# First feed-forward of a diffusion layer: quad weight pieces prepared in pairs in a written-out order, dot tiles loaded one piece ahead, SiLU rows kept in DRAM

## The chip, the cores and the metric

The kernel runs on 1 core of one Trainium2 chip. The metric is the device time of one execution in microseconds. The kernel before took 2806.91 us as the median of 3 runs (2805.06 to 2813.4).

## The reference, cut to what matters

The program is one layer on 256 latent and 256 context tokens of width 2048: a half-step SwiGLU, a token mixer (attention and a long convolution), and a second half-step SwiGLU. Each is modulated by shifts, scales and gates from one linear map `w_ada` of SiLU(c) for the latent tokens and of SiLU(c_ctx) for the context tokens.

```python
D_MODEL, SEQ, CTX_LEN, D_FF, N_MOD = 2048, 256, 256, 5632, 9

def half_ffn(s, m, slot, g, w_up, w_down):
    h = modulate(rms_norm(s, g), chunk(m, 3 * slot), chunk(m, 3 * slot + 1))
    gate, up = jnp.split(h @ w_up, 2, axis=-1)
    return s + 0.5 * chunk(m, 3 * slot + 2) * ((silu(gate) * up) @ w_down)

mod = (silu(c) @ w_ada + b_ada)[:, None, :]          # 9 chunks of 2048
mod_c = (silu(c_ctx) @ w_ada + b_ada)[:, None, :]
x = half_ffn(x, mod, 0, g_norm[0], w_ffn1_up, w_ffn1_down)
ctx = half_ffn(ctx, mod_c, 0, g_norm[0], w_ffn1_up, w_ffn1_down)
...                                                  # token mixing, then the second half_ffn on x
```

All values are 32-bit floats. The change lies in the two `half_ffn` lines of slot 0 (the first ff) and in the `w_ada` products that are computed beside them.

## The kernel before, in words

**Products in two parts.** A float operand is split into a high part `hi` (a cast to the matmul format fp32r, on ScalarE) and a remainder `lo = raw - hi` (on VectorE). One product of blocks is then three matmuls: hi by hi, hi by lo, lo by hi (`mm3`, L239 to L241). `split_to` (L208 cast, L209 remainder) and `weight` (L228 cast, L232 remainder) make the parts.

**The up loop.** The columns of `w_up` are worked in 44 steps j of 128 gate and 128 up columns. Steps 0 to 2 (the wave) run first, beside the start of the kernel. Steps 3 to 43 are `Ffn.up` (from 240 us to 1165 us in the profile nearly all of this loop). A step takes its 16 blocks of the inner dimension in four pieces kq of 4 blocks, each loaded as a tile `raw` of 128 x 1024 floats, 512 KB (`weight_load`, L216, SP's queue, 4 buffers).

- Piece kq = 0 is always plain. Its weights are cast into tiles `u` (L418, L419), and its remainder is made by an accumulating DMA from POOL's queue (L420). From j = 4 on its raw tile is `plain`, with one buffer. It is prepared one step ahead, after the products of kq = 1 of the step before.
- Pieces kq = 3, 2, 1 become quad pieces from j = 5, 7, 9 on. A quad piece computes its 2 x 2 x 2 block products with seven products instead of eight, on tokens of one stream (256 columns, where a plain product has both, 512). Its products come in two parts: first three products per block pair on the raw weights' first three blocks (the plain part, tiles `bhi`, `blo`, 128 x 768, 2 buffers each in the pool `adap`), then four on sums of the weights (the summed part, tiles `whi`, `wlo`, 128 x 1024, 3 buffers each). So a quad piece has 2 x 7 x 3 = 42 matmuls of 256 columns, and a plain piece 4 x 2 x 3 = 24 of 512.
- In `prepare`, a quad piece is made in this order: bhi (ScalarE), blo (VectorE), three in-place sums on `raw` (L426, L427, L428, VectorE), whi (ScalarE), wlo (VectorE).

At the end of a step its sums are combined on VectorE (L474 to L481, with a SiLU at L480 on ScalarE) into one tile of activations, and `keep` (L484 on) stores it to DRAM as a high part and a remainder: a cast, a negated copy, two stores and an accumulating store, all from POOL's queue (L489, L490, L491).

**The dots.** The products with `w_ada` that are not needed at once are made on VectorE: a tile `adaw` of 128 x 1024 weights (512 KB, L141, SP's queue) is multiplied by a SiLU row `crow`, replicated on all partitions, and summed along the row (L145). Columns 5 to 8 of the nine (`ADA_UP`, 128 dots) run in the up loop with 2 buffers, columns 2 to 4 (`ADA_DOWN`, two rows each) in the down loop with 4. `ada_hook` is called after each piece and adds a rate of 0.79 dots per call in the up loop; the load and its dot are written one right after the other (`ada_dve`). A load stands behind the latest weight load on SP's queue.

**The rows.** `open_dots` loads a row of 2048 floats of c into all partitions (1 MB, L896, ScalarE's queue) and applies SiLU there (L897, 128 x 2048): one row before the up loop, two before the down loop.

**The down loop** (about 1165 to 1700 us) reads the activations back (L506, POOL's queue) in groups of four j, from group 9 on, then 8, 10 and the others, with weights from `w_dn` (24 plain products per step).

**What sets the order.** The program is written in one sequence; the build gives each engine its own queue and may set an instruction earlier or later than its place in the text where its inputs allow. `tc.issue_after(x)` sets what is written inside it behind x on x's engine. Each engine and each DMA-issuing queue works its list in order. In the trace of before, for instance, the first dots run before the wave's activations, behind which they are written.

Of the kernel before, what the change touches and what calls it, by code (L numbers as in the profile page):

```python
# [14 lines left out]
ALU = mybir.AluOpType  # L15
# [47 lines left out]
def hybrid_layer_kernel(ctx: ExitStack, tc: tile.TileContext, a):  # L63
# [14 lines left out]
    def U(shape, dt=F32):  # L78
        return T(up, shape, "u", dt, 58)
# [50 lines left out]
    warm = mod[0][8][:, 0:1]  # L130
    S.activation(warm, ones[:, 0:1], AF.Silu)

    def ada_dve(c, d, b):
        n = c * KT + d
        t = T(adap, (P, D // 2), "adaw", bufs=adaw_bufs)
        src = a["w_adaT"][n, :, b * (D // 2) : (b + 1) * (D // 2)]
        if last_load[0] is None:
            nc.scalar.dma_start(t, src)
        else:
            with tc.issue_after(last_load[0].ins):  # L140
                nc.sync.dma_start(t, src)  # L141
        for i in range(2 if c < 5 else 1):
            sc = T(adap, (P, D // 2), "adas", mybir.dt.bfloat16, bufs=1)
            mcol = mod[i][c][:, d : d + 1]
            V.tensor_tensor_reduce(  # L145
                out=sc, in0=t, in1=crow[i][:, b * (D // 2) : (b + 1) * (D // 2)], scale=1.0,
                scalar=mcol if b else bada[:, n : n + 1], op0=ALU.mult, op1=ALU.add, accum_out=mcol,
            )

    def ada_finish(c, d0, d1):  # L150
        for i in range(2 if c < 5 else 1):
# [200 lines left out]
    class Ffn:  # L352
        def __init__(self, wup, wdown, cm, hook=None):
            self.wup, self.wdown, self.cm = wup, wdown, cm
            self.hook = hook or (lambda: None)
            self.h = [None] * KT
            self.mm = mm3
            self.held = {}
            self.sums, self.first = {}, {}
            self.wupq = a["w_up1q"]  # L360

        def open(self, alt=False):
# [47 lines left out]
        def prepare(self, j, kq):  # L410

            pool = adap if kq == 0 and j > WAVE else None
            raw = weight_load(self.wupq[j - WAVE, kq], (P, 2, 4, P), pool=pool)
            out = []
            if kq == 0:
                hi, lo = ([U((P, 4, P), F32R) for _ in range(2)] for _ in range(2))
                for q in range(2):
                    S.copy(hi[q], raw[:, q])  # L418
                    S.activation(lo[q], hi[q].bitcast(F32), AF.Copy, scale=-1.0)  # L419
                    nc.gpsimd.dma_start(lo[q], raw[:, q].bitcast(F32R), accum_op=ALU.add)  # L420
                return [(hi, lo)]
            if not self.quads(j, kq):
                return [weight(None, (P, 2, 4, P), raw=raw)]
            for n in (3, 4):
                if n == 4:
                    V.tensor_sub(raw[:, :, 0:4:3], raw[:, :, 3:4].broadcast_to((P, 2, 2, P)), raw[:, :, 0:3:2])  # L426
                    V.tensor_sub(raw[:, :, 2], raw[:, :, 2], raw[:, :, 0])  # L427
                    V.tensor_sub(raw[:, :, 1], raw[:, :, 1], raw[:, :, 2])  # L428
# [20 lines left out]
        def up(self, j):  # L449
# [2 lines left out]
            total = list(left)  # L452
            banks = [(PA, PB)[j % 2]((P, 2, L)) if n else None for n in left]
            for kq in range(4):
                w = self.prepare(j, kq) if kq else self.ahead
# [107 lines left out]
    NF = 64  # L563
    dram = ctx.enter_context(tc.tile_pool(name="dram", bufs=1, space=bass.MemoryType.DRAM))
    spec = [T(dram, (P, 2, L), f"spec{i}") for i in range(8)]
    actd = [T(dram, (P, 2, 2, L), f"act{j}", F32R) for j in range(JT)]

    def filter_spectrum():
# [108 lines left out]
    def ada_next():  # L677
        if done[0] < len(todo):
            c, d, b = todo[done[0]]
            ada_dve(c, d, b)  # L680
            done[0] += 1
            if b == 1:
                ada_finish(c, d, d + 1)

    def ada_hook():
        owed[0] += rate[0]
        while owed[0] >= 1.0:
            owed[0] -= 1.0
            ada_next()

    steps = filter_spectrum()
    load = None
# [196 lines left out]
    def open_dots(n, bufs):  # L889
        nonlocal adap, adap_cm, adaw_bufs  # L890
        adap_cm = tc.tile_pool(name="adap", bufs=2)
        adap, adaw_bufs = adap_cm.__enter__(), bufs
        crow.clear()
        for i in range(n):
            crow.append(T(adap, (P, D), f"crow{i}", bufs=1))
            nc.scalar.dma_start(crow[i], a["crow"][i : i + 1, :].partition_broadcast(P))  # L896
            S.activation(crow[i], crow[i], AF.Silu)  # L897

    adap = adap_cm = adaw_bufs = None
    open_dots(1, 2)  # L900

    xs = [[None] * (KT // 2) for _ in range(2)]
    build = f1.build()
# [2 lines left out]
    for j in range(WAVE, JT):  # L906
        f1.up(j)
        if j == WAVE:
            f1.hook = lambda: (next(build, None), ada_hook())
    rs1 = U((P, 2, L))  # L910
    cont, lat = [], []

# [3 lines left out]

    more = mix_input(1, cont, PASSES[-1][0], PA)
    norm_plan = iter(NORM_PLAN)
    while done[0] < len(ADA_UP) * KT * 2:
        ada_next()  # L920
    adap_cm.__exit__(None, None, None)
    open_dots(2, 4)
    owed[0] = -4.0

    def down_hook(p):
# [6 lines left out]
    while done[0] < len(todo):  # L932
        ada_next()
    last_load[0] = None
    adap_cm.__exit__(None, None, None)


    mp_cm = tc.tile_pool(name="mp", bufs=1)
# [671 lines left out]
```

## Time and profile before

| | |
|---|---|
| runs, median (range) | 2806.91 us (2805.06 to 2813.4) |
| the profiled execution | 2812.43 us |
| its span | 2810.7 us |
| granted TensorE clock, mean | 0.983 |
| DMA, mean over the span | 217 GB/s |
| issues of the up loop's raw, plain and dot tiles (each 512 KB, whole page) | 124, 40 and 223 |

The profile is of one execution. PE is TensorE's matmuls, PEld its weight loads, DVE VectorE, ACT ScalarE, POOL GpSimd, SP SyncE; "SPq" and the like is the engine's queue that issues DMAs. "L145" is a line of the kernel. In a group or a timeline row, "wlo<-raw,whi" names what is written and what is read; "x110" is a count; behind the bar or in brackets stands the time that the engine was idle just before, and what ended it. A line of waits gives the total in us, the number of times and the longest. The view of one line or tile gives shortest, median and longest duration in ns, and when the first and the last of them started.

### The profile page before, as it was taken

The page shows a single profiled execution, that of the slowest core. Times are in us where ns is not written, and L with a number is a line of the kernel's source. Part 1 is how long each engine was busy: PE and PEld are TensorE (multiplying, and loading weights), DVE is VectorE, ACT ScalarE, POOL GpSimd, SP SyncE. Part 2 cuts the span into 40 slices and gives each one's busy share as a digit, 9 for nine tenths or more (in the row PEclk, how much of TensorE's full clock was granted, in tenths as well). Part 3 has the DMA queues.
Part 4 walks back from the last instruction along what each step waited for, and adds up shares of the span by engine and source line. Part 5 has one row for each costly group of instructions (what it writes and reads, how often), then busy time and mean ns, then how long its engine had stood idle before and what let it go on. Part 6 is the DMA issues. An engine that isn't in the chain of part 4 may idle for free.

```text
span 2810.7 us, 37981 instructions
## 1 busy us (share of the span) xinstructions
PE 2653.9 (94%) x14480; PEld 2255.6 (80%) x14480; DVE 1914.2 (68%) x3050; ACT 1112.7 (40%) x1546; POOL 253.5 (9%) x394
## 2 busy tenths in 40 slices
PE   8999888898989988799999999999999999999999
PEld 5677788887878888687887798888878888888887
DVE  6756777767777767577897769688875545554444
ACT  5343333433433334311121145546554444444333
POOL 1121111111111111232001000000000000000000
PEclk9999999999999999899999999999999999999999
DMA  9976677777776777899678756633556666666665
GB/s 370 349 218 190 192 210 213 220 207 203 192 227 190 207 205 214 288 376 314 242 251 296 256 178 178 187 113 124 187 166 191 189 188 189 189 192 203 202 202 157
DMA packets 194146, 608.94 MB, mean 217 GB/s; under 512 B 22315, under 2 KB 25324, under 8 KB 189484
## 3 DMA queue, kind: packets, MB, share of 16 engines
q1 hardware_dynamic: 140012, 501.77, 54.2%
q0 software_dynamic: 53184, 100.95, 15.1%
q10 hardware_dynamic: 768, 3.80, 0.3%
q8 instruction: 113, 1.85, 0.3%
q14 instruction: 69, 0.57, 0.1%
HBM read 546.13 MB, written 38.81 MB: 208 GB/s over the span
## 4 chain that ended last, share of the span: by engine, by line
PE 53%; issue 22%; DMA 14%; DVE 7%; POOL 3%; ACT 1%; SPq 0%; POOLq 0%; DVEq 0%; ACTq 0%
PE pa L1270 9%; PE pa L1271 9%; PE pa L1269 9%; DMA adaw<-in_w_adaT_dram 6%; PE pa L247 3%; DMA act<-u 3%; PE pb L241 3%; PE pb L239 3%; PE pb L240 3%; DVE adas L145 2%; PE pa L239 2%; PE pa L240 2%; PE pa L241 2%; DMA u<-plain 2%; PE pa L249 2%
## 5 line engine op out<-in xcount | busy, mean ns | idle before, releaser
L232 DVE TENSOR_TENSOR wlo<-raw,whi 128x1024 fp32r<-128x1024 f32 x487 | 595.0, 1223 | 415.6 <-ACT whi L228 414.2
L228 ACT CAST whi<-raw 128x1024 fp32r<-128x1024 f32 x487 | 511.9, 1052 | 882.9 <-PE pa L1271 413.4
L1269 PE MATMUL pa<-whi,u 128*128 128x512 f32 x1060 | 414.1, 391 | 0.6 <-ACT whi L228 0.6
L1270 PE MATMUL pa<-wlo,u 128*128 128x512 f32 x1060 | 412.9, 390 | 0.5 <-DVE wlo L232 0.5
L1271 PE MATMUL pa<-whi,u 128*128 128x512 f32 x1060 | 412.9, 390 | 0.0
L239 PE MATMUL pa<-u,whi 128*128 128x256 f32 (+1 forms) x928 | 318.3, 344 | 32.9 <-ACT whi L208 21.5
L241 PE MATMUL pa<-u,wlo 128*128 128x256 f32 (+1 forms) x928 | 316.2, 341 | 24.1 <-DVE wlo L209 20.6
L241 PE MATMUL pb<-u,wlo 128*128 128x256 f32 (+1 forms) x920 | 310.8, 338 | 23.1 <-DVE wlo L209 14.5
L239 PE MATMUL pb<-u,whi 128*128 128x256 f32 (+1 forms) x920 | 311.2, 338 | 17.2 <-ACT whi L208 17.1
L240 PE MATMUL pa<-u,whi 128*128 128x256 f32 (+1 forms) x928 | 314.2, 339 | 4.5 <-DMA u<-act 4.1
L240 PE MATMUL pb<-u,whi 128*128 128x256 f32 (+1 forms) x920 | 307.7, 334 | 0.0
L145 DVE CUSTOM_DVE_ANT_0 adas<-adaw,crow,mod 128x1024 bf16<-128x1024 f32 x160 | 205.2, 1283 | 130.7 <-DMA adaw<-in_w_adaT_dram 128.3
L145 DVE CUSTOM_DVE_ANT_0 adas<-adaw,crow,cond 128x1024 bf16<-128x1024 f32 x160 | 205.1, 1282 | 127.2 <-DMA adaw<-in_w_adaT_dram 116.4
L208 ACT CAST whi<-raw 128x1024 fp32r<-128x1024 f32 x111 | 116.3, 1048 | 430.5 <-DVE raw L428 430.5
L1270 PEld LDWEIGHTS pa<-wlo,u 128*128 128x128 f32 x1060 | 199.1, 188 | 41.8 <-DVE wlo L232 1.0
L1269 PEld LDWEIGHTS pa<-whi,u 128*128 128x128 f32 x1060 | 199.0, 188 | 41.7 <-ACT whi L228 1.1
L1271 PEld LDWEIGHTS pa<-whi,u 128*128 128x128 f32 x1060 | 199.0, 188 | 41.3
L239 PEld LDWEIGHTS pa<-u,whi 128*128 128x128 f32 x928 | 180.1, 194 | 60.2 <-ACT whi L208 24.6
L241 PEld LDWEIGHTS pa<-u,wlo 128*128 128x128 f32 x928 | 180.5, 195 | 47.4 <-DVE wlo L209 25.5
L241 PEld LDWEIGHTS pb<-u,wlo 128*128 128x128 f32 x920 | 179.0, 195 | 46.6 <-DVE wlo L209 19.3
L239 PEld LDWEIGHTS pb<-u,whi 128*128 128x128 f32 x920 | 178.9, 194 | 37.8 <-ACT whi L208 20.2
L240 PEld LDWEIGHTS pa<-u,whi 128*128 128x128 f32 x928 | 180.5, 195 | 23.4 <-DMA u<-act 5.7
(353 smaller groups left out, 4725.0 us busy)
## 6 DMA issues: line engine op xcount, KB each, us to landing
adaw<-in_w_adaT_dram SPq DMA_DIRECT2D x223, 512.0 KB, 5.8
raw<-in_w_dn_dram SPq DMA_DIRECT2D x184, 512.0 KB, 3.7
raw<-in_w_up_dram SPq DMA_DIRECT2D x176, 512.0 KB, 3.6
raw<-in_w_up1q_dram SPq DMA_DIRECT2D x124, 512.0 KB, 5.4
u<-act POOLq DMA_DIRECT2D x136, 256.0 KB, 9.0
act<-u POOLq DMA_DIRECT2D x132, 256.0 KB, 3.8
wrow<-in_w_ada_dram SPq DMA_DIRECT2D x32, 1024.0 KB, 9.7
plain<-in_w_up1q_dram SPq DMA_DIRECT2D x40, 512.0 KB, 3.7
```

Source lines behind the costliest of these rows:

```text
L145: V.tensor_tensor_reduce(out=sc, in0=t, in1=crow[i][:, b * (D // 2) : (b + 1) * (D // 2)], scale=1.0, scalar=mcol if b else bada[:, n : n ...
L208: S.copy(hi, src)
L228: S.copy(hi, raw)
L232: V.tensor_sub(lo, raw, hi.bitcast(F32))
L239: PE.matmul(ps, w[0], xx[0], start=start, stop=False)
L240: PE.matmul(ps, w[0], xx[1], start=False, stop=False)
L241: return PE.matmul(ps, w[1], xx[0], start=False, stop=stop)
L247: PE.matmul(ps, w[0], x, start=start, stop=stop)
L249: PE.matmul(ps[:, 0, :], w[1], x[:, 0, :], start=False, stop=False)
L1269: PE.matmul(ps[t], hi, w[0], start=start, stop=False)
L1270: PE.matmul(ps[t], hi, w[1], start=False, stop=False)
L1271: last = PE.matmul(ps[t], lo, w[0], start=False, stop=stop)
```

## The change

Four things change.

1. **Quad pieces in pairs.** `prepare` returns the raw tile of a quad piece, and the new `quad_weights` does the rest. For a piece n it also begins the next quad piece n+1, perhaps of the next step: its load, its plain cast and its plain remainder. The order is given: on ScalarE the plain cast of n+1, then the summed cast of n; on VectorE the plain remainder of n+1, then the summed remainder of n, then the sums of n+1.
2. **Dots one piece behind their loads.** `ada_hook` issues the load; the dot is written at the next call, and behind the latest summed (or plain) remainder on VectorE (`last_lo`). The buffers stay 2 and 4. The hook makes no more than the up loop's 128 loads there; what is left is done by `dots_rest`.
3. **SiLU rows in DRAM.** Both rows are loaded once as a 32 x 128 tile (POOL's queue), one SiLU is applied, and they are stored to `silu_rows` in DRAM (POOL's queue). The replicated rows are read from there on SP's queue: row 0 once before the up loop, kept through the down loop, row 1 before the down loop.
4. **The last activation.** `keep` of j = 43 makes its parts by a cast and a VectorE remainder and stores them with two plain stores.

The core of the diff ("..." marks what is left out):

```diff
-    def ada_dve(c, d, b):
+    last_lo = [None]
+    waiting = []
+
+    def dot_load(c, d, b):
...
         if last_load[0] is None:
-            nc.scalar.dma_start(t, src)
+            nc.sync.dma_start(t, src)
...
+    def dot(t, c, d, b):
         for i in range(2 if c < 5 else 1):
...
+        if b == 1:
+            ada_finish(c, d, d + 1)
...
-            V.tensor_sub(lo, raw, hi.bitcast(F32))
+            last_lo[0] = V.tensor_sub(lo, raw, hi.bitcast(F32))
...
-            for n in (3, 4):
-                if n == 4:
-                    V.tensor_sub(raw[:, :, 0:4:3], raw[:, :, 3:4].broadcast_to((P, 2, 2, P)), raw[:, :, 0:3:2])
-                    V.tensor_sub(raw[:, :, 2], raw[:, :, 2], raw[:, :, 0])
-                    V.tensor_sub(raw[:, :, 1], raw[:, :, 1], raw[:, :, 2])
-                if n == 3:
-                    hi, lo = (T(adap, (P, 2, n, P), name, F32R, 2) for name in ("bhi", "blo"))
-                else:
-                    hi, lo = (T(wp, (P, 2, n, P), name, F32R, 3) for name in ("whi", "wlo"))
-                out.append(split_to(raw[:, :, 0:n], hi, lo))
-            return out
+            return raw
+
+        def plain_part(self, raw):
+            hi, lo = (T(adap, (P, 2, 3, P), name, F32R, 2) for name in ("bhi", "blo"))
+            return raw, hi, lo, S.copy(hi, raw[:, :, 0:3])
+
+        def remainder(self, raw, hi, lo):
+            return V.tensor_sub(lo, raw[:, :, 0:3], hi.bitcast(F32))
...
+        def quad_weights(self, j, kq):
+            if self.begun is None:
+                raw, hi, lo, _ = self.plain_part(self.prepare(j, kq))
+                self.remainder(raw, hi, lo)
+                self.sums_of(raw)
+                self.begun = raw, hi, lo
+            raw, hi, lo = self.begun
...
+            if n < JT * 4:
+                nraw, nhi, nlo, cast = self.plain_part(self.prepare(n // 4, n % 4))
+            thi, tlo = (T(wp, (P, 2, 4, P), name, F32R, 3) for name in ("whi", "wlo"))
+            with ExitStack() as order:
+                if cast is not None:
+                    order.enter_context(tc.issue_after(cast.ins))
+                S.copy(thi, raw)
+            if cast is not None:
+                rem = self.remainder(nraw, nhi, nlo)
+            with ExitStack() as order:
+                if cast is not None:
+                    order.enter_context(tc.issue_after(rem.ins))
+                last_lo[0] = V.tensor_sub(tlo, raw, thi.bitcast(F32))
+            if cast is not None:
+                then(last_lo[0], self.sums_of, nraw)
+                self.begun = nraw, nhi, nlo
+            return [(hi, lo), (thi, tlo)]
...
         def keep(self, j, act):
+            if j == JT - 1:
+                for s_, t in enumerate(split(act, (P, 2, L))):
+                    nc.gpsimd.dma_start(actd[j][:, s_], t)
+                return
...
+    def dots_due(keep):
+        while len(waiting) > keep:
+            t, step = waiting.pop(0)
+            with ExitStack() as order:
+                if last_lo[0] is not None:
+                    order.enter_context(tc.issue_after(last_lo[0].ins))
+                dot(t, *step)
+
     def ada_hook():
+        behind = len(waiting)
         owed[0] += rate[0]
-        while owed[0] >= 1.0:
+        while owed[0] >= 1.0 and done[0] < len(todo):
             owed[0] -= 1.0
-            ada_next()
+            dots_due(adaw_bufs - 1)
+            behind = min(behind, len(waiting))
+            waiting.append((dot_load(*todo[done[0]]), todo[done[0]]))
+            done[0] += 1
+        dots_due(len(waiting) - behind)
...
+    rows = T(up, (2 * KT, P), "mt", bufs=3)
+    nc.gpsimd.dma_start(rows, a["crow"].rearrange("i (k p) -> (i k) p", p=P))
     f1.ahead = f1.prepare(WAVE, 0)
     for j in range(WAVE):
         f1.close(j, wave[j])
+    S.activation(rows, rows, AF.Silu)
+    nc.gpsimd.dma_start(silu_rows.rearrange("i k p -> (i k) p"), rows)
...
+    def row_in(pool, i):
+        crow.append(T(pool, (P, D), f"crow{i}", bufs=1))
+        nc.sync.dma_start(crow[i], silu_rows[i : i + 1].rearrange("i k p -> i (k p)").partition_broadcast(P))
```

More of the change, by code (lines that the diff above doesn't have):

```diff
@@ L141, in ada_dve @@
                 nc.sync.dma_start(t, src)
+        return t
+    def dot(t, c, d, b):
         for i in range(2 if c < 5 else 1):
@@ L358, in __init__ @@
             self.held = {}
-            self.sums, self.first = {}, {}
+            self.sums, self.first, self.begun = {}, {}, None
             self.wupq = a["w_up1q"]
@@ L413, in prepare @@
             raw = weight_load(self.wupq[j - WAVE, kq], (P, 2, 4, P), pool=pool)
-            out = []
             if kq == 0:
@@ L434, in prepare, with sums_of @@
-            return out
+            return raw
[4 more added lines that the diff above has]
+            return V.tensor_sub(lo, raw[:, :, 0:3], hi.bitcast(F32))
+        def sums_of(self, raw):
+            V.tensor_sub(raw[:, :, 0:4:3], raw[:, :, 3:4].broadcast_to((P, 2, 2, P)), raw[:, :, 0:3:2])
+            V.tensor_sub(raw[:, :, 2], raw[:, :, 2], raw[:, :, 0])
+            return V.tensor_sub(raw[:, :, 1], raw[:, :, 1], raw[:, :, 2])
@@ new lines, in quad_weights @@
+        def quad_weights(self, j, kq):
[5 more added lines that the diff above has]
+            raw, hi, lo = self.begun
+            self.begun = None
+            n = j * 4 + kq + 1
+            while n < JT * 4 and not self.quads(n // 4, n % 4):
+                n += 1
+            cast = summed = None
+            if n < JT * 4:
[15 more added lines that the diff above has]
+            return [(hi, lo), (thi, tlo)]
@@ L454, in up @@
             for kq in range(4):
-                w = self.prepare(j, kq) if kq else self.ahead
+                w = self.ahead if kq == 0 else self.quad_weights(j, kq) if self.quads(j, kq) else self.prepare(j, kq)
                 for bank, part, n, q, block, x in todo[kq]:
@@ L565, in hybrid_layer_kernel @@
     spec = [T(dram, (P, 2, L), f"spec{i}") for i in range(8)]
+    silu_rows = T(dram, (2, KT, P), "silu_rows")
     actd = [T(dram, (P, 2, 2, L), f"act{j}", F32R) for j in range(JT)]
@@ L675, in hybrid_layer_kernel, with ada_hook, dots_rest @@
     owed, rate = [0.0], [0.0]
[L677 to L680, printed above, removed]
-            done[0] += 1
[L682 to L686, printed above, removed]
-        while owed[0] >= 1.0:
-            owed[0] -= 1.0
-            ada_next()
+    def dots_due(keep):
[5 more added lines that the diff above has]
+                dot(t, *step)
+    def ada_hook():
+        behind = len(waiting)
+        owed[0] += rate[0]
+        while owed[0] >= 1.0 and done[0] < len(todo):
+            owed[0] -= 1.0
+            dots_due(adaw_bufs - 1)
+            behind = min(behind, len(waiting))
+            waiting.append((dot_load(*todo[done[0]]), todo[done[0]]))
+            done[0] += 1
+        dots_due(len(waiting) - behind)
+    def dots_rest(end):
+        while done[0] < end:
+            dots_due(adaw_bufs - 1)
+            waiting.append((dot_load(*todo[done[0]]), todo[done[0]]))
+            done[0] += 1
+        dots_due(0)
     steps = filter_spectrum()
@@ L885, in hybrid_layer_kernel @@
         f1.close(j, wave[j])
+    S.activation(rows, rows, AF.Silu)
+    nc.gpsimd.dma_start(silu_rows.rearrange("i k p -> (i k) p"), rows)
     rowp_cm.__exit__(None, None, None)
     crow = []
[L889 to L900, printed above, removed]
+    rows_cm = tc.tile_pool(name="rows", bufs=1)
+    rows_pool = rows_cm.__enter__()
+    def row_in(pool, i):
+        crow.append(T(pool, (P, D), f"crow{i}", bufs=1))
+        nc.sync.dma_start(crow[i], silu_rows[i : i + 1].rearrange("i k p -> i (k p)").partition_broadcast(P))
+    row_in(rows_pool, 0)
+    adap_cm = tc.tile_pool(name="adap", bufs=2)
+    adap, adaw_bufs = adap_cm.__enter__(), 2
     xs = [[None] * (KT // 2) for _ in range(2)]
@@ L908, in hybrid_layer_kernel @@
         if j == WAVE:
-            f1.hook = lambda: (next(build, None), ada_hook())
+            f1.hook = lambda: (next(build, None), ada_hook() if done[0] < len(ADA_UP) * KT * 2 else None)
     rs1 = U((P, 2, L))
@@ L918, in hybrid_layer_kernel @@
     norm_plan = iter(NORM_PLAN)
-    while done[0] < len(ADA_UP) * KT * 2:
-        ada_next()
+    dots_rest(len(ADA_UP) * KT * 2)
     adap_cm.__exit__(None, None, None)
-    open_dots(2, 4)
+    adap_cm = tc.tile_pool(name="adap", bufs=2)
+    adap, adaw_bufs = adap_cm.__enter__(), 4
+    row_in(adap, 1)
     owed[0] = -4.0
@@ L931, in hybrid_layer_kernel @@
     next(downs)
-    while done[0] < len(todo):
-        ada_next()
+    dots_rest(len(todo))
     last_load[0] = None
     adap_cm.__exit__(None, None, None)
+    rows_cm.__exit__(None, None, None)
     mp_cm = tc.tile_pool(name="mp", bufs=1)
```

2 lines of the change are left out of this document (1 added, 1 removed).

## The prediction, made before the change was run

> **What bounds the kernel now.** I read the page first, then the stretches, then the waits of each engine inside the longest stretch, last one turn of its loop.
>
> ```profile
> PE 2653.9 (94%) x14480; PEld 2255.6 (80%) x14480; DVE 1914.2 (68%) x3050; ACT 1112.7 (40%) x1546; POOL 253.5 (9%) x394
> ```
>
> ```profile
> 175.00:240.00 65.00, 60.26 (x277) 49.58 (x276) 34.10 (x56) 21.10 (x32) 9.46 (x13) 0.97 0.72 202
> 240.00:1165.00 925.00, 822.40 (x5579) 755.96 (x5577) 674.32 (x1109) 361.34 (x531) 143.23 (x192) 0.97 0.73 206
> 1165.00:1230.00 65.00, 51.73 (x210) 40.68 (x209) 41.72 (x69) 14.85 (x14) 24.51 (x46) 0.87 1.10 376
> 1230.00:1700.00 470.00, 455.22 (x2163) 381.24 (x2162) 366.47 (x589) 113.36 (x130) 47.57 (x90) 0.99 0.78 262
> ...
> 2200.00:2810.70 610.70, 605.67 (x2704) 501.12 (x2702) 301.40 (x285) 248.19 (x269) 0.00 (x0) 1.00 0.61 190
> ```
>
> The first line is the page's: TensorE 94% busy as a mean. The second fence is the table of stretches (length, then busy time of PE, PEld, DVE, ACT, POOL, the granted clock, DMA share, GB/s). The up loop of the first ff is 240 to 1165: PE is idle there for 925 - 822.4 = 102.6 us. From 1230 on it is idle for 14.8, and at the end for 5.0. The change touches the first three rows and the fourth; what is to be won lies in the second.
>
> How long would the loop be if PE never waited?
>
> ```profile
> 905.03 0.28 PE L240 MATMUL pb<-u,bhi 128*128 128x256 f32 x1
> ...
> 906.84 0.28 PE L240 MATMUL pb<-u,bhi 128*128 128x256 f32 x1
> ```
>
> ```profile
> L474 DVE TENSOR_TENSOR mt<-sq,pb x20: 411/416/421, 239.2 to 1164.2; 128x256 f32<-128x256 f32 x20
> L474 DVE TENSOR_TENSOR mt<-sq,pa x19: 411/414/418, 264.4 to 1149.4; 128x256 f32<-128x256 f32 x19
> ```
>
> Fifteen 256-column matmuls lie between those two starts without a wait: 1.81 / 15 = 0.121 us each. A 512-column one costs 610.70 / 2704 = 0.226 in the last stretch, which is nearly all such. A quad piece is 42 of the first kind (5.07 us), a plain block of four 24 of the second (5.42). A j from 9 on has three quad pieces and one plain: 20.6 us; j = 6 has 21.3, j = 7 and 8 have 21.0. L474 runs once per quad-bearing j, 39 times, so 38 turns take 1164.2 - 239.2 = 925 us, 24.3 each. The floor is 35 x 20.6 + 21.3 + 42 = 784 us. So 141 us are lost here (more than the 102.6, since a matmul behind a stall is drawn longer).
>
> Who makes PE wait, and what makes that engine late:
>
> ```profile
> PE pa L239 <- ACT whi L208: 21.5, 15, 5.7
> PE pa L241 <- DVE wlo L209: 20.6, 21, 2.3
> ```
>
> ```profile
> DVE adas L145 <- DMA adaw<-in_w_adaT_dram: 156.5, 51, 7.9
> DVE wlo L209 <- ACT whi L208: 65.6, 60, 1.2
> DVE blo L209 <- ACT bhi L208: 13.6, 14, 2.6
> ```
>
> These are the waits of PE and of DVE in 240 to 1165 (total, times, longest). For the pa banks (every second j) alone, 42.1 us of PE's idle time are for the high and low tiles of summed quads. DVE is busy 674.3 us and waits 235.7 in three named ways: 910 of 925. It is the loop's bound, though 73% busy: its queue is worked in order, and a dot product (L145) whose tile has not landed holds the sums and remainders behind it. One turn shows it, of DVE, ACT and SP:
>
> ```profile
> 896.12 0.69 DVE L426 TENSOR_TENSOR raw<-raw 128x512 f32<-128x512 f32 x1
> 902.82 1.28 DVE L145 CUSTOM_DVE_ANT_0 adas<-adaw,crow,cond 128x1024 bf16<-128x1024 f32 x1 [6.01 <-DMA adaw<-in_w_adaT_dram]
> ```
>
> ```profile
> 906.14 1.05 ACT L208 CAST whi<-raw 128x1024 fp32r<-128x1024 f32 x1 [11.19 <-DVE raw L428]
> ```
>
> ```profile
> 897.50 0.33 SPq L216 DMA_DIRECT2D plain<-in_w_up1q_dram  x1
> 897.88 0.90 SPq L141 DMA_DIRECT2D adaw<-in_w_adaT_dram  x2
> ```
>
> The dot's load leaves SP right behind the plain load; DVE stands 6 us between the first and second sum of a piece, and ACT waits 11 us for the third.
>
> **The change part by part.** *Order of a quad piece.* Nothing is added or removed per piece: two casts, two remainders, three sums. Their groups in the loop, DVE's and ACT's (busy, mean ns, idle before):
>
> ```profile
> L209 DVE TENSOR_TENSOR wlo<-raw,whi 128x1024 fp32r<-128x1024 f32 x110 | 134.7, 1224 | 67.1 <-ACT whi L208 65.6
> L209 DVE TENSOR_TENSOR blo<-raw,bhi 128x768 fp32r<-128x768 f32 x108 | 103.0, 954 | 14.4 <-ACT bhi L208 13.6
> L145 DVE CUSTOM_DVE_ANT_0 adas<-adaw,crow,mod 128x1024 bf16<-128x1024 f32 x59 | 75.6, 1282 | 78.9 <-DMA adaw<-in_w_adaT_dram 78.6
> L145 DVE CUSTOM_DVE_ANT_0 adas<-adaw,crow,cond 128x1024 bf16<-128x1024 f32 x59 | 75.6, 1281 | 78.0 <-DMA adaw<-in_w_adaT_dram 77.9
> L426 DVE TENSOR_TENSOR raw<-raw 128x512 f32<-128x512 f32 x108 | 74.7, 691 | 3.2
> L427 DVE TENSOR_TENSOR raw<-raw 128x256 f32<-128x256 f32 x108 | 45.7, 423 | 2.7
> L428 DVE TENSOR_TENSOR raw<-raw 128x256 f32<-128x256 f32 x108 | 45.6, 422 | 2.1
> ```
>
> ```profile
> L208 ACT CAST whi<-raw 128x1024 fp32r<-128x1024 f32 x109 | 114.2, 1048 | 430.5 <-DVE raw L428 430.5
> L208 ACT CAST bhi<-raw 128x768 fp32r<-128x768 f32 x108 | 89.1, 828 | 3.9 <-PE pa L240 3.9
> ```
>
> Today the five steps of one piece are a chain through two engines: 0.83 + 0.95 + 1.54 + 1.05 + 1.22 = 5.6 us, longer than PE's 5.07 for a piece. After the change ACT casts piece n+1's plain part and then piece n's summed part, whose sums were made a step ago; DVE takes remainder n+1, remainder n, sums n+1. The chain from PE's release of a bhi buffer (two of them: the plain part of n-1) to wlo of n is 0.83 + 1.05 + 1.22 = 3.1 us, while PE still has 5.07 us of n-1's summed and n's plain part to do. Cover of 2 us; the 65.6 + 13.6 us of DVE waits go. DVE needs 0.95 + 1.22 + 1.54 = 3.7 us per piece and about one dot (1.28): 5.0 of 5.07, so nothing is spare inside the three pieces; what is left over is taken in the 5.4 us of the plain block. The wait that is added: whi of n, and all of ACT behind it, stands behind the cast of n+1, which needs raw n+1 landed. That load is asked for one piece earlier in the program (0.33 us of SP), but leaves, as now, when a raw buffer comes free.
>
> *Dots one piece behind their loads.* They keep their number, 128 by the code, and their cost. The two rows show 2 x 59 here, so 10 ran before 240; tied behind the latest wlo, at most these 10 move into the loop: 13 us more, 687 in all, 18.1 per turn against 20.6 of PE. Behind a waiting dot on DVE stand the next remainder and the closing of a j.
>
> ```profile
> adaw<-in_w_adaT_dram SPq DMA_DIRECT2D x121, 512.0 KB, 5.7
> raw<-in_w_up1q_dram SPq DMA_DIRECT2D x108, 512.0 KB, 5.4
> ...
> crow<-in_crow_dram ACTq DMA_DIRECT2D x2, 1024.0 KB, 9.9
> ```
>
> A load lands 5.7 us after issue (DMA view of the same stretch); one piece is 5.07, or 5.4 for the plain block. So of today's 3.1 us per stall (156.5 / 51) most goes, and under 1 us per dot stays where the load leaves with no lead beyond the piece. From 0 (landed in time) to 3.1 (as now); I take under 0.8, the point at which DVE (18.1 + 3.2 dots x 0.8) reaches PE's 20.6, because the load gains a whole piece. Quicker turns also press the same bytes into less time: DMA share 0.73 x 24.3 / 21 = 0.84, below the 1.10 of the boundary row.
>
> *Sum for the loop.* Floor 784, plus 0.5 us per turn for a queue run at 90% whose waits I cannot see (bounds 0, and 1.9 if half of today's 141 / 38 stays): 803. Gain 122.
>
> *The silu rows.* Three row broadcasts (1 MB each) with a SiLU of 128 x 2048 become one small SiLU, a 16 KB store and two broadcasts, moved from ACT's to SP's queue. SP must hold the first read until the store is done, and the weight loads queued behind it with it: POOL's store takes its turn behind the wave's stores. At its dearest that is about one broadcast, 9.9 us; PE was idle 4.7 us in 175 to 240 with four raw buffers ahead. I take 0, bounds -5 and +5. The Trainium skill's page "DMA: Bandwidth & Descriptors", section "Rules for kernel authors", says that a DMA which reads what another wrote must wait on that one's completion semaphore; it speaks against this part, and if the whole 9.9 us fell on PE the sum would be 10 us worse. No run yet shows this pair.
>
> *The boundary, and the last act.*
>
> ```profile
> 1176.58 0.79 PE L239 MATMUL pa<-u,whi 128*128 128x512 f32 x1 [8.54 <-DMA u<-act]
> ```
>
> ```profile
> 1170.03 1.91 ACT L897 ACTIVATE crow<-crow 128x2048 f32<-128x2048 f32 x1 [2.75 <-DMA crow<-in_crow_dram]
> ```
>
> PE waits 8.5 us for act tiles while the DMA engines run at 376 GB/s. One of two 1 MB rows goes (1 MB / 376 GB/s = 2.8 us), two SiLUs (1.9 each) leave ACT, and the last act loses its accumulating third transfer for a DVE remainder. I take 5 us of the 13.3 idle (65 - 51.7); bounds 0 and 13. *Down loop:* the dots come behind the wlo of their step; 5 of the 14.8 us idle, bounds -5 and 14. *The second ff:* not touched.
>
> Sum: 122 + 0 + 5 + 5 = 132. The profiled execution took 2812.43 us (span 2810.7 and 1.7 around it), 0.2% above the runs' median of 2806.91. Forecast 2812.4 - 132 = 2680 us.
>
> **The rivals.** *Dots still wait.* Only the order helps:
>
> ```profile
> SPq L216 <- DVE wlo L209: 409.1, 82, 9.9
> SPq L216 <- DMA u<-plain: 167.2, 37, 10.0
> ```
>
> The plain load holds SP 4.5 us a time (167.2 / 37) for its single buffer, and dot loads stand behind it; if that eats the piece gained, DVE keeps its 156.5: 687 + 157 + 19 = 863, gain 62, with the other 10 gives 2740. Against: the load has five more us, and one stall per turn is all the plain load makes. Chance 0.17; here too belongs that the build queues the dots much as before.
>
> *Nothing waits.* Loop at 784: gain 141 + 10, 2661. For: 20.6 - 18.1 = 2.5 us of slack per turn. Against: inside the pieces DVE has none. Chance 0.10. The page "Perfetto Trace Analysis" of the Trainium skill, section "Identifying the Most-Contended Engine", would judge TensorE by its weight loads' busy share instead: 756 of 925 us, so the loop could shrink to 756 and the whole to about 2633. The pace of the undisturbed matmuls above does not bear that out.
>
> *Slower: raw tiles come late.* The cast of n+1 now goes ahead of whi of n. If raw n+1 was queued on SP behind the plain load's 4.5 us and lands 5.4 later, that is 9.9, less 5.4 covered by the plain block: 4.5 us of PE per turn, 171 in 38, on 803: 974, 49 worse than now; less 10 elsewhere, 2851. It decides once a raw load leaves SP under 5.4 us ahead of its cast. Against: a raw buffer is freed by the wlo of four pieces before, which leaves two pieces, 10 us. Chance 0.07. *Gains and waits cancel:* near 2810, chance 0.04.
>
> **How the numbers follow.** Forecast 0.62, between 2655 and 2705. Faster by over 0.3% (about what a measurement here can tell from no change): 0.62 + 0.10 + 0.17 = 0.89; same 0.04; slower 0.07. The range holds the first three: low 2650 (floor, with most of the boundary), high 2750 (dots still wait, and the outer terms at nothing).
>
> **What would show it.** Right: 38 turns of L474 in about 803 us (21.1 each); DVE's wait for adaw in the loop under 60 us in total and for whi near none; PE idle in the loop under 45; ACT's whi no longer behind L428. Wrong: adaw waits over 120 us (the dots), ACT's bhi waiting for raw's DMA (the late tiles), or SP holding weights behind crow near 180 us. A loop at 21 us per turn with the total unmoved would mean the time is given back in the down loop.

## The result, and the profile after

The changed kernel took 2657.59 us (median of 4 runs, 2655.05 to 2661.02) where the kernel before took 2805.99 (4 runs beside it): ratio 0.9466, 95% interval 0.9447 to 0.9486. The profiled execution took 2656.8 us, 155.6 less than the 2812.43 of before. Forecast was 2680, range 2650 to 2750.

The page's line of busy times of the kernel after:

```profile
PE 2606.0 (98%) x14480; PEld 2238.3 (84%) x14480; DVE 1892.0 (71%) x3051; ACT 1114.4 (42%) x1543; POOL 253.8 (10%) x395
```

To compare stretches, they are cut where as many matmuls have been recorded in both kernels (columns as in the prediction's table of stretches): the up loop is 5575 matmuls, the boundary 218, the down loop 2165. Before:

```profile
240.10:1163.90 923.80, 821.36 (x5575) 755.45 (x5574) 673.55 (x1107) 361.05 (x531) 142.67 (x191) 0.97 0.73 206
1163.90:1231.10 67.20, 53.77 (x218) 42.05 (x217) 43.49 (x71) 15.14 (x15) 25.59 (x47) 0.87 1.10 375
1231.10:1701.40 470.30, 455.52 (x2165) 381.46 (x2164) 366.16 (x589) 114.08 (x131) 47.04 (x89) 0.99 0.77 262
```

After:

```profile
233.70:1038.30 804.60, 784.53 (x5575) 741.92 (x5574) 643.84 (x1091) 363.19 (x523) 145.30 (x196) 0.99 0.82 235
1038.30:1096.50 58.20, 53.37 (x218) 42.51 (x217) 38.07 (x62) 10.84 (x12) 19.13 (x37) 0.91 1.13 395
1096.50:1547.30 450.80, 447.85 (x2165) 378.62 (x2164) 374.49 (x603) 114.17 (x131) 48.02 (x91) 1.00 0.82 275
```

The loop gives 119.2 of the 155.6 us, the boundary 9.0, the down loop 19.5, the start 6.4 (240.1 - 233.7); 1.5 are elsewhere. The 6.4 at the start can't be put down to a part of the change: in e4 below, whose edit lies at the end of the loop, the loop begins at 240.8 again. In the loop, TensorE's idle time falls from 102.4 to 20.1 us, and its busy time by 37 as well, though the matmuls are the same: their granted clock rose from 0.97 to 0.99.

The waits of DVE in the loop after (total, times, longest), beside the 156.5, 65.6 and 13.6 of before:

```profile
DVE wlo L471 <- ACT whi L465: 65.0, 74, 1.7
DVE blo L439 <- ACT bhi L436: 42.8, 31, 3.4
DVE adas L151 <- DMA adaw<-in_w_adaT_dram: 38.9, 17, 6.2
```

The dots' wait is down to a quarter. The two waits for ScalarE's casts, which the prediction had going away, are still there and together larger.

The 38 turns of the loop, by the first combining operation of a step (L515 after, L474 before):

```profile
L515 DVE TENSOR_TENSOR mt<-sq,pb x20: 410/414/422, 221.7 to 1043.1; 128x256 f32<-128x256 f32 x20
```

They take 1043.1 - 221.7 = 821.4 us by this measure, against 925 of before. In before the first of them had been held up (it ran at 239.2, behind a ScalarE copy that began at 236.55 though its last matmul was issued at 223.3), so the matmul counts are the fairer comparison. From start to start of these operations, 32 turns take 20.8 us on average, close to the prediction's 20.6 without a wait. Five take 25.6, 27.0, 27.2, 26.0 and 26.1 us, together 29 us over 20.6, and the last 25.0. What ends the one of 26.0 (841.2 to 867.2), on DVE, ACT and PE:

```profile
860.54 0.15 DVE L164 TENSOR_SCALAR mod<-mod 128x1 f32<-128x1 f32 x1
865.68 1.28 DVE L151 CUSTOM_DVE_ANT_0 adas<-adaw,crow,cond 128x1024 bf16<-128x1024 f32 x1 [4.99 <-DMA adaw<-in_w_adaT_dram]
866.89 0.08 DVE L151 DVE_READ_ACCUMULATOR2_ANT mod<- 128x1 f32 x1
866.89 0.42 DVE L444 TENSOR_TENSOR raw<-raw 128x256 f32<-128x256 f32 x1
```

```profile
867.34 1.05 ACT L465 CAST whi<-raw 128x1024 fp32r<-128x1024 f32 x1 [5.60 <-DVE raw L444]
```

```profile
870.69 0.39 PE L249 MATMUL pa<-u,wlo 128*128 128x256 f32 x1 [1.14 <-DVE wlo L471]
...
877.63 0.38 PE L247 MATMUL pa<-u,whi 128*128 128x256 f32 x1 [1.89 <-ACT whi L465]
...
878.89 0.58 PE L249 MATMUL pa<-u,wlo 128*128 128x256 f32 x1 [0.76 <-DVE wlo L471]
```

It is the picture of before, seldom now: a dot stands in DVE's queue for a tile that has not landed, between the second and the third sum (L443, L444) of a piece; ScalarE waits 5.6 us for that third sum; TensorE waits 1.14, 1.89 and 0.76 us in the next two pieces. There are five dot waits of 4.6 to 6.2 us in the loop (dots at 329.7, 584.4, 715.5, 865.7, 995.3). The load of the dot at 865.7, on SP's queue:

```profile
859.98 0.33 SPq L224 DMA_DIRECT2D plain<-in_w_up1q_dram  x1
860.40 0.39 SPq L144 DMA_DIRECT2D adaw<-in_w_adaT_dram  x1
```

It left 0.42 us behind a plain load that had held the queue for 5.3 us, until its single buffer came free. The loads of the other four late dots do the same: each leaves some 0.4 us behind a plain load that had waited 6.2 to 7.6 us. These turns also stand out by their number of dots. At 0.79 per call and four calls per turn, 3.16 dots fall to a turn: of the 38 turns seven have four dots, the others three (one has two), and the five long turns and the last are six of those seven.

### The profile page after: what moved, and what is told of

It reads as the page before. It is cut to its first block, busy times and chain, and to the rows that moved or that the text cites. A ratio compares the mean times of both kernels' runs of the same rounds, so it can differ in the third digit from the quotient of the medians.

```text
span 2655.0 us, 38017 instructions
## 1 busy us (share of the span) xinstructions
PE 2606.0 (98%) x14480; PEld 2238.3 (84%) x14480; DVE 1892.0 (71%) x3051; ACT 1114.4 (42%) x1543; POOL 253.8 (10%) x395
## 3 DMA queue, kind: packets, MB, share of 16 engines
q1 hardware_dynamic: 140444, 504.40, 57.1%
## 4 chain that ended last, share of the span: by engine, by line
PE 78%; issue 9%; DMA 5%; DVE 4%; ACT 2%; POOL 1%; SPq 0%; POOLq 0%; DVEq 0%; ACTq 0%
PE pa L1331 10%; PE pa L1332 10%; PE pa L1330 10%; PE pa L247 6%; PE pa L248 6%; PE pa L249 6%; PE pb L247 6%; PE pb L249 6%; PE pb L248 6%; PE pa L255 3%; DMA act<-u 2%; PE pa L257 2%; PE pa L1044 1%; PE pa L1045 1%; DMA adaw<-in_w_adaT_dram 1%
## 5 line engine op out<-in xcount | busy, mean ns | idle before, releaser
L236 ACT CAST whi<-raw 128x1024 fp32r<-128x1024 f32 x487 | 512.4, 1053 | 881.4 <-PE pa L1332 413.4
L249 PE MATMUL pb<-u,wlo 128*128 128x256 f32 (+1 forms) x920 | 305.1, 332 | 7.4 <-DVE wlo L471 7.3
L247 PE MATMUL pb<-u,whi 128*128 128x256 f32 (+1 forms) x920 | 306.6, 334 | 4.6 <-ACT whi L465 4.5
L248 PE MATMUL pb<-u,whi 128*128 128x256 f32 (+1 forms) x920 | 304.5, 331 | 0.0
L247 PEld LDWEIGHTS pb<-u,whi 128*128 128x128 f32 x920 | 176.5, 192 | 23.0 <-ACT whi L465 5.6
L248 PEld LDWEIGHTS pb<-u,whi 128*128 128x128 f32 x920 | 176.6, 192 | 15.7 <-issue 0.4
```

The lines of the kernel that those rows point to most:

```text
L247: PE.matmul(ps, w[0], xx[0], start=start, stop=False)
L248: PE.matmul(ps, w[0], xx[1], start=False, stop=False)
L249: return PE.matmul(ps, w[1], xx[0], start=False, stop=stop)
```

## The experiments

The theory after the result: the dots' lead is the gain, because a dot whose tile is late holds everything behind it in DVE's in-order queue. The written order of casts and remainders is not the gain, and may even leave pieces no room to run ahead. Rivals: the order gives about half; the rows or the last activation give the boundary; the dots' work, not their waiting, was the burden.

| run | what it is | median us | ratio to before, 95% | loop of 5575 matmuls, us |
|---|---|---|---|---|
| after | | 2657.59 | 0.9466 (0.9447 to 0.9486) | 804.6 |
| e1 | order of pieces alone | 2797.38 | 0.9957 (0.9943 to 0.9971) | 923.9 |
| e2 | dots' lead alone | 2641.02 | 0.9399 (0.9381 to 0.9416) | 789.9 |
| e3 | after, rows as before | 2663.55 | 0.9479 (0.9459 to 0.9499) | 808.2 |
| e4 | after, last act as before | 2658.48 | 0.9458 (0.9439 to 0.9477) | 808.7 |
| b1 | before, narrow dots | 2787.49 | 0.9926 (0.9912 to 0.9941) | 905.5 |
| e5 | after, order not written out | 2629.69 | 0.9360 (0.9348 to 0.9373) | 780.7 |
| e12 | e5 and the order of casts | 2650.10 | 0.9429 (0.9415 to 0.9442) | 791.7 |
| e13 | e5 and the order of remainders | 2639.87 | 0.9390 (0.9376 to 0.9403) | 781.6 |
| e11 | e5, dots not ahead of their loads | 2733.69 | 0.9729 (0.9712 to 0.9745) | 885.6 |
| e7 | after, dot loads free of plain | 2656.89 | 0.9461 (0.9447 to 0.9476) | 802.0 |
| e10 | e2, dot loads free of plain | 2635.15 | 0.9384 (0.9372 to 0.9397) | 784.2 |
| e14 | e5, dot loads free of plain | 2623.78 | 0.9339 (0.9325 to 0.9352) | 779.8 |

The loops of e2, e3, e10, e11 and e13 hold 5574 recorded matmuls. Each loop time is that of one profiled execution.

**e1, the order alone.** Pairs in the written order, rows and last activation as after; each load is followed at once by its dot, which is tied to nothing.

```diff
+    def dots_now(end):
+        while done[0] < end:
+            step = todo[done[0]]
+            dot(dot_load(*step), *step)
+            done[0] += 1
...
-            waiting.append((dot_load(*todo[done[0]]), todo[done[0]]))
+            dots_now(done[0] + 1)
```

> The kernel after with the dots as before: each dot is written right behind its load, tied to nothing, in the up and in the down loop; the quad pieces keep their new order. Theory (VectorE's queue is the sum of its work and its waits, and both halves of the change take waits out of it): the loop falls back to 687 busy + 157 of waiting for dot tiles + 19 = 863 us against the 805 that the kernel after shows, the down loop gives back its 19, so about 2735 us; VectorE waits over 100 us for adaw in the loop. Rival 1 (the order of the pieces is all that counts): the loop stays near 805 and only the down loop returns, about 2677. Rival 2 (the dots are all that counts): about 2795, near the kernel before.

Measured 2797.38, near what was expected if the dots are all that counts. The loop is as long as before (923.9 against 923.8), and DVE's wait for dots no shorter:

```profile
DVE adas L151 <- DMA adaw<-in_w_adaT_dram: 165.2, 42, 8.1
DVE wlo L471 <- ACT whi L465: 44.1, 63, 1.1
```

```profile
237.70:1161.60 923.90, 831.84 (x5575) 778.40 (x5574) 660.74 (x1099) 359.16 (x528) 146.93 (x199) 0.94 0.73 206
```

The wait for the summed cast shrinks by 21.5 us, as the order intends, and nothing comes of it: what leaves one place of DVE's queue turns up at the dots (156.5 to 165.2) and the plain remainders (13.6 to 41.8). TensorE is idle 92.1 us, 10 less than before, but its granted clock is 0.94 against 0.97, and its busy time is 10 us longer. The 11 us that the run gains stand at the boundary (56.5 against 67.2).

**e2, the dots alone.** The lead of the dots, with the pieces prepared as in before; rows and last activation as after.

```diff
-            raw, hi, lo = self.begun
...
+            raw, hi, lo, _ = self.plain_part(self.prepare(j, kq))
+            self.remainder(raw, hi, lo)
+            self.sums_of(raw)
...
+            S.copy(thi, raw)
+            last_lo[0] = V.tensor_sub(tlo, raw, thi.bitcast(F32))
```

> The kernel after with each quad piece prepared by itself in the old order (plain cast, plain remainder, sums, summed cast, summed remainder); the dots stay one piece behind their loads. Theory: the chain of 5.6 us per piece against PE's 5.07 comes back, 0.55 us x 108 pieces = 59 us less what the plain block covers; about 2700 us (2685 to 2715). Rival 1 (the order is all that counts): about 2780. Rival 2 (the dots are all that counts): within 8 us of the kernel after's 2657.

Measured 2641.02, below what the theory and both rivals gave: it beats the whole change, by 17 us. DVE's waits in its loop:

```profile
DVE wlo L453 <- ACT whi L452: 73.5, 83, 1.5
DVE adas L151 <- DMA adaw<-in_w_adaT_dram: 22.9, 19, 4.4
DVE blo L439 <- ACT bhi L436: 16.3, 17, 2.6
```

The waits for casts are no shorter than before (65.6 and 13.6), and TensorE is idle 13 us in 789.9. So these waits cost next to nothing once the dots no longer stand: the in-order chain of a piece, 5.6 us long by the prediction's sum, does not hold a loop whose pieces take 5.07. Steps of neighbouring pieces must overlap. The lead was run only together with the tie behind the latest remainder; what it is worth without that tie stays open.

**e3 and e4, the rows and the last activation.** e3 loads and activates replicated rows as before, e4 keeps the accumulating store for j = 43:

```diff
+            nc.scalar.dma_start(crow[i], a["crow"][i : i + 1, :].partition_broadcast(P))
+            S.activation(crow[i], crow[i], AF.Silu)
```

```diff
-            if j == JT - 1:
-                for s_, t in enumerate(split(act, (P, 2, L))):
-                    nc.gpsimd.dma_start(actd[j][:, s_], t)
-                return
```

> The kernel after with the rows loaded as before: a 1 MB replicated row on ScalarE's queue and a SiLU on 128 x 2048, once before the up loop, twice before the down loop; no SiLU rows in DRAM. Theory: worth little, about 4 us, at the boundary of up and down loop: 2661 us. Rival (the rows made the 6 us gained before 240 us and most of the 9 at the boundary): 2670 us or more. Other rival (the store and the read back cost as much as they save): 2657.

> The kernel after with the activation of j = 43 stored as the others (cast, negated copy, two stores and an accumulating store). Theory: group 10 is used third, its last tile is needed some 40 us later, so nothing: 2657 to 2659 us. Rival (the accumulating store on POOL's queue holds the fetches behind it): 3 to 8 us more, seen as PE waiting for act tiles at the boundary.

Both intervals overlap that of after: by the medians the rows are worth 6 us and the last activation 1, and neither can be told from nothing. Neither gives the boundary back: it is 58.6 in e3 and 58.0 in e4.

**b1, the dots' work.** Before, with each dot of the up loop multiplying 8 of its 1024 columns; loads, waits and count are unchanged, the products are left incomplete.

```diff
-                out=sc, in0=t, in1=crow[i][:, b * (D // 2) : (b + 1) * (D // 2)], scale=1.0,
+                out=sc, in0=t[:, 0:w_], in1=crow[i][:, b * (D // 2) : b * (D // 2) + w_], scale=1.0,
```

> The kernel before, where a dot of the up loop works on 8 of its 1024 columns (its sums are then wrong): VectorE's work falls by some 118 x 1.2 = 140 us in the loop, every load and every wait for it stays. Theory (the waiting, not the work, of the dots holds the loop): VectorE has 674 - 140 busy, so it catches up faster after each stall, but the stall of up to 6 us per turn still stands in front of the sums: gain of 20 to 60 us, about 2765. Rival (VectorE is short of time): the loop goes to its floor, about 2665.

Measured 2787.49, 22 us under the kernel before beside it (2809.18), at the low end of the 20 to 60 expected. Its loop, and DVE's two largest waits in it:

```profile
238.80:1144.30 905.50, 818.44 (x5575) 756.66 (x5574) 553.94 (x1101) 363.39 (x530) 146.96 (x199) 0.97 0.74 210
```

```profile
DVE adas L146 <- DMA adaw<-in_w_adaT_dram: 156.0, 74, 8.2
DVE blo L210 <- ACT bhi L209: 103.3, 28, 3.8
```

DVE's busy time falls by 673.6 - 553.9 = 120 us and the loop by 18; the wait for tiles stays, 156.0 against 156.5, and most of the time set free turns up as waits for plain casts (103.3 against 13.6). It is the standing, not the multiplying, that bound the loop.

**e5, e12, e13: what the written order costs.** e5 prepares in pairs as after but leaves out both `issue_after` and the tie of the sums, so that the build may place casts, remainders and sums. e12 puts back the tie on ScalarE alone, e13 that on VectorE alone.

```diff
-            with ExitStack() as order:
-                if cast is not None:
-                    order.enter_context(tc.issue_after(cast.ins))
-                S.copy(thi, raw)
+            S.copy(thi, raw)
...
-                    order.enter_context(tc.issue_after(rem.ins))
...
-                then(last_lo[0], self.sums_of, nraw)
+                self.sums_of(nraw)
```

> The kernel after, where a quad piece still begins the next one, but the order of its casts, remainders and sums is left to the build (no edges written). The dots alone gave 2641 us, with pairs in the written order it is 2657. Theory now: the written order costs the 16 us, because the summed cast of a piece must stand behind a plain cast that waits for PE to free a bhi buffer; without it 2640 to 2648 us. Rival (the pairing itself costs it, by which raw tile is held and how SP's queue comes to stand): 2655 to 2660.

> The kernel after with the written order kept on ScalarE alone (summed cast of n behind the plain cast of n+1); VectorE's order is left to the build. With both it is 2657 us, with neither 2630. Theory: the plain cast of n+1 needs a bhi buffer that PE frees only at the end of the plain part of n-1, so a summed cast tied behind it can lead PE by no more than one piece (5 us), too little to ride over a dot that waits 5 to 6 us, while three whi buffers would allow more; this one edge is enough: 2645 to 2660. Rival (VectorE's edges cost it): 2630 to 2636.

> The kernel after with the written order kept on VectorE alone (summed remainder of n behind the plain remainder of n+1, sums of n+1 behind that); ScalarE's order is left to the build. Theory: the same limit by the other road, since the plain remainder of n+1 also needs the bhi buffer's release: 2645 to 2660. Rival (only ScalarE's edge costs): 2630 to 2636.

e5 took 2629.69, 28 us under after and lower than expected. Its loop:

```profile
233.30:1014.00 780.70, 774.87 (x5575) 733.75 (x5574) 657.35 (x1091) 361.33 (x523) 144.54 (x196) 1.00 0.85 243
```

TensorE is idle 6 us. What the build does with its freedom shows on ScalarE and DVE near 845 us of e5, where TensorE works on a plain block:

```profile
844.37 1.05 ACT L462 CAST whi<-raw 128x1024 fp32r<-128x1024 f32 x1 [1.52 <-DVE raw L444]
845.32 0.37 ACT L508 COPY sq<-pb 128x256 f32<-128x256 f32 x1
845.89 1.05 ACT L462 CAST whi<-raw 128x1024 fp32r<-128x1024 f32 x1 [0.20 <-DVE raw L444]
```

```profile
846.11 1.22 DVE L465 TENSOR_TENSOR wlo<-raw,whi 128x1024 fp32r<-128x1024 f32 x1
...
848.23 1.22 DVE L465 TENSOR_TENSOR wlo<-raw,whi 128x1024 fp32r<-128x1024 f32 x1
```

Two summed parts are made one after the other, with no plain cast between: two pieces of lead, 10 us of TensorE's work. The written order forbids that: the summed cast of n stands behind the plain cast of n+1, and that one needs a `bhi` buffer, of which there are two; the one that it takes comes free when TensorE has done the plain part of n-1. That this limit is what costs the time is argued from the program and this stretch; ScalarE's tie alone bears it out, VectorE's doesn't. e12 costs 20 us by the medians, as expected, 11 of them in the loop of its profile. e13 costs 10, between theory and rival, and its loop is hardly longer than e5's:

```profile
233.60:1015.20 781.60, 775.82 (x5574) 735.34 (x5573) 643.70 (x1090) 362.12 (x523) 144.71 (x195) 1.00 0.84 241
```

Its boundary is longer instead (60.4 us against 56.0). That profile is of the fastest of e13's four runs. Together the two ties cost 28 us, 24 of them in the loop.

**e11, the lead of one piece.** e5 with load and dot written together, still tied behind the latest remainder.

```diff
-        behind = len(waiting)
...
-        dots_due(len(waiting) - behind)
+            dots_due(0)
```

> The fastest kernel so far (pairs, order unwritten, 2630 us) with each dot written right behind its load again, but still tied behind the latest summed or plain remainder. Theory: the tie alone keeps the build from setting a dot ahead of the sums, but its load then leaves only about one dot ahead of it: most of the gain stays, VectorE's wait for dot tiles rises from 20 us to 60 or more, 2640 to 2680 us. Rival 1 (the piece of lead is what counts): above 2740. Rival 2 (the tie is all): within 5 us of 2630.

Measured 2733.69: 104 us worse than e5 and close to rival 1, so the tie alone is not enough. DVE's dot wait in its up loop:

```profile
DVE adas L151 <- DMA adaw<-in_w_adaT_dram: 116.4, 34, 6.6
```

Its down loop, however, takes 449.4 us, all of the gain there, and there is none in e1 (469.2), where the dots are not tied. So in the down loop the tie suffices, and in the up loop the piece of lead is needed. The dots have four buffers there and two here; the loops differ in more than that, and no run changed the number of buffers alone.

**e7, e10, e14: dot loads free of the plain load.** Here the load of `plain` isn't recorded as the latest weight load, so that the program no longer ties a dot's load behind it; added to after, e2 and e5.

```diff
-        if done[0]:
+        if done[0] and pool is None:
```

> The kernel after, where a dot's load is tied behind the latest raw load but no longer behind the plain load of the next step. Theory: in the loop of the kernel after five turns take 25.6 to 27.2 us instead of 20.5, each with a dot that waited 5 to 6 us for a tile whose load had left SP right behind a plain load; without the tie these go: 16 to 25 us less, 2632 to 2641, and no wait of a dot over 3 us. Rival (the written order is what costs): it stays within 5 us of 2657, the stalls merely move.

> The kernel with the dots behind their loads and the old order of a quad piece (2641 us), and also without the tie behind the plain load. Its loop is at 789 us, 5 above the floor of 784 worked out from the kernel before, and PE waits there for plain remainders, hardly for VectorE. Theory: nothing left for this edit: 2641 within 4. Rival: the 23 us for which VectorE still waits for dot tiles reach PE after all: 2630.

> The fastest kernel so far (2630 us) where, besides, a dot's load is not tied behind the plain load. With the old order of a quad piece this gave 6 us (2641 to 2635). Theory: the loop stands at its floor of 784 us already, so nothing: 2627 to 2632. Rival: 6 us here too, 2624.

It is worth nothing in after (2656.89, as the rival said), where five dot waits of 4.3 to 5.9 us remain. But the order on SP's queue has not changed at these places. Of the dot at 865.5 in e7:

```profile
860.06 0.33 SPq L224 DMA_DIRECT2D plain<-in_w_up1q_dram  x1
860.48 0.40 SPq L144 DMA_DIRECT2D adaw<-in_w_adaT_dram  x1
```

In all five the load still leaves some 0.4 us behind a plain load. So e7 doesn't test whether the plain load in front of the dot's load makes the long turns. In e2 and e5 the edit is worth 6 us by the medians (between the two expectations in e10, as the rival said in e14), with intervals that overlap; in e10 the loop is 6 us shorter, in e14 the boundary is 7 (49.0 against 56.0 in e5), which e11 shows as well (49.0) without this edit, so its place isn't settled. e14 has the lowest median: 6.6% under before and 34 us under after.

## Why the prediction was right or wrong, point by point

**The bound** was read rightly: DVE's in-order queue, with the dots standing in it. e1, e2 and b1 show it from three sides.

**The floor** of 784 us for 38 turns holds: no loop went below it. e5's loop of 780.7 us has 5575 of the 5628 matmuls counted in the floor (42 per quad piece, 24 per plain one), so it is to be set against 784 less 53 x 0.137 (20.6 / 150) = 777: 4 us over.

**Dots one piece behind their loads.** Right: "under 1 us per dot stays" was 38.9 / 118 = 0.33 (118 loads in the loop, landing after 5.8 us), and the wait is under the 60 that was named. But the stay is uneven, five stands of about 5 us (26.9 of the 38.9), and these cost time.

**Order of a quad piece.** This step failed. "Cover of 2 us; the 65.6 + 13.6 us of DVE waits go": they stayed, 65.0 + 42.8 us. ScalarE's waits in the loop of after:

```profile
ACT whi L465 <- DVE raw L444: 112.3, 61, 6.8
ACT bhi L436 <- PE pa L248: 59.1, 38, 3.3
ACT bhi L436 <- PE pb L248: 57.1, 35, 2.9
```

The prediction took the sums of a piece as made "a step ago", and named as a sign that ScalarE's summed cast no longer waits for the third sum. It still does, 61 times (99 times and 430.5 us before). The plain cast waits 73 times for TensorE to free a `bhi` buffer, and DVE then stands before that cast as well. The cover of 2 us was right as a sum, but it is no cover against a DVE that stands 5 us at a dot, and by the program the same two `bhi` buffers that start the chain forbid a larger one. The waits that the order was to remove were harmless beside the dots' (e2 has them too). The order was counted as an aid; by e5 it costs 28 us.

**Sum for the loop.** 803 forecast, 804.6 measured, for another reason than given, so that the agreement is in part luck: 0.5 us per turn was meant as an even loss, and it is nearly all in five turns. By the prediction's own sign, the 38 turns from L474 to L474 (L515), it is 821.4. For the one shown, the three turns from 841.2 on take 26.0 + 21.2 + 22.0 = 69.2 us, 7.4 over three of 20.6; of these, 1.14 + 1.89 + 0.76 = 3.8 are TensorE's waits, and about 1.5 are lost where its matmuls ran at half pace for 3.4 us (below); the other 2 are not accounted for.

**The silu rows.** 0 within 5, right within what e3 can tell. No hold of SP is to be seen; POOL's store and the read on SP:

```profile
152.83 0.53 POOL L948 DMA_DIRECT2D silu_rows<-mt  x1 [1.89 <-ACT mt L947]
```

```profile
155.78 0.33 SPq L224 DMA_DIRECT2D raw<-in_w_up1q_dram  x1
156.20 0.38 SPq L956 DMA_DIRECT2D crow<-silu_rows  x1
156.67 0.38 SPq L224 DMA_DIRECT2D raw<-in_w_up1q_dram  x1
```

The store lands 3.1 us after its issue, about when SP comes to the read. The rule of the Trainium skill's page "DMA: Bandwidth & Descriptors", section "Rules for kernel authors", that a read of DRAM which another DMA wrote must wait for its completion, costs nothing visible here.

**The boundary** gained 9.0 (5 forecast, 13 at most). That the gain comes from the rows or the last activation is not borne out: e3 and e4 each keep it. Whether either one suffices, or another part makes it, stays open; no run undid both. Part of it may come from earlier: b1, which has none of the four parts, stands at 63.4 us against 67.2.

**Down loop.** 19.5 us, where 5 was taken and 14 the bound: mis-sized. The bound was TensorE's drawn idle time of 14.8, and a matmul behind a stall is drawn longer, as the prediction itself had said of the up loop: busy time fell by 7.7 us too. e1 and e11 put the gain on the tie of the dots.

**The rivals.** "Dots still wait" gave the order 62 us; e1, which has the order, the rows and the last activation, gains 11 in all, none of it in the loop. But its reason, that a dot's load stands behind a plain load which holds SP, is what the five long turns show. "Nothing waits" (2661) is nearest in the total, but its loop of 784 is e5's, not after's. The measured total lies 22 us under the forecast of 2680, though the loop came out as forecast: down loop, start and boundary gave 35 where 10 was taken. "Raw tiles come late": no wait of ScalarE for raw's DMA appears in the loop of after; bhi waits for TensorE's buffers instead (59.1 and 57.1 us for the pa and pb steps). The rule of the Trainium skill's page "Perfetto Trace Analysis", section "Identifying the Most-Contended Engine", made a loop of 756 from the weight loads' busy time; e5 and e14 end at 780, where the weight loads' own busy time has fallen to 734, so before's 756 us were no floor. The rule would also have passed over DVE, 73% busy: 910 of its 925 us were work or standing in queue.

**Open:** why only the written order has dot stands of 5 us five times in the loop. The turn with four dots and the plain load in front of the dot's load are common to the five, but e5 has turns with four dots too, and none of its stands in the loop is above 2.5 us; e13 has one of 5.8. No run moved the plain load, or changed the rate of the dots.

## What to carry to other kernels

On an engine with an in-order queue, count the time that it stands at operands still on their way as its own load: an engine 73% busy bound this loop, and taking 120 us of its work away shortened the loop by 18 (b1), while a tie and one piece of lead for its dots shortened it by 134 (e2). Write such a consumer a step behind its load, not right after it. An order written out by hand can limit how far the work runs ahead (here it cost 28 us): measure it against the same program without the order.

## What the runs showed of the hardware

In after, waits of less than 2 us close together were followed by half a clock. Three stretches of after around the waits shown above (granted clock third from the end):

```profile
871.00:874.90 3.90, 3.90 (x35) 3.90 (x34) 2.80 (x6) 2.43 (x5) 0.81 (x2) 1.00 0.38 134
878.90:882.30 3.40, 3.40 (x16) 3.40 (x17) 3.35 (x7) 0.02 (x1) 0.83 (x1) 0.51 1.03 173
882.50:886.00 3.50, 3.50 (x32) 3.50 (x31) 2.64 (x3) 1.49 (x2) 0.00 (x0) 1.00 0.96 277
```

Right after waits of 1.89 and 0.76 us with two matmuls between them, 3.4 us run at 0.51: 16 matmuls take what 28 would at 0.121 us each. The Trainium skill's page "TensorE: Matmul & The Clock Gate", Part 1, puts the half clock after at least one idle window of about 3.4 us; here the two waits add up to 2.65. The loop of after has five such stretches of 3.4 us at half clock, one in the turn after each of the five long ones; four follow the same two waits, one follows waits of 0.29 and 1.74 us. The loop of before has eight, of 3.4 or 6.8 us and 47.8 us in all, during or right after single waits of 2.4 to 5.7 us. TensorE is busy for 39.1 us of them, so some 20 us of before were lost to half pace on top of the waits themselves (an estimate); in e5 and e14 the mean clock of the loop is 1.00.
